# Modulation sums for two blocks over all features, in place of four blocks over half of them, and the first norm and products by pairs of blocks

## The chip, the cores and the metric

One Trainium2 chip, one of its cores. The metric is the time of one execution on the device in microseconds (us); smaller is better. Three runs of the kernel before took 2045.69, 2046.32 and 2048.83 us, median 2046.32.

## The reference, cut to what matters

A backbone of two layers over 512 latent and 256 context tokens with 1024 features each. Each layer turns a conditioning vector into six modulation vectors per stream (latent and context), and uses the first two to shift and scale the normed tokens before one wide projection:

```
mod_x = silu(c)     @ ada_w[layer] + ada_b[layer]      # ada_w: 1024 x 6144
mod_c = silu(c_ctx) @ ada_w[layer] + ada_b[layer]
sh1, sc1, g1, sh2, sc2, g2 = split(mod, 6)             # 1024 = 8 blocks of 128 features each
u = (rms_norm(x, norm1_g) * (1 + sc1) + sh1) @ w_in    # all three mixers read u
x = x + g1 * (mixers(u) @ w_out)
x = x + g2 * experts(rms_norm(x, norm2_g) * (1 + sc2) + sh2)
```

The mixers are a Fourier group, a bidirectional chunkwise mLSTM and a latent attention; the experts are a choice of 16. All is computed in 32 bits.

## The kernel before, in words

Tokens lie with features on the partitions: eight blocks of 128 features by 768 tokens, two blocks to a tile (`XB = 2`, tiles X0 to X3). The program is one long trace of instructions; a planner with a cost model of its own puts them into one queue per engine, by program order among what it takes to be ready, and each engine then works its queue in order. Transfers from memory are issued by SyncE's queue, in order too.

*The modulation.* `ada_w` is 24 MB a layer and is read in pieces of 1 MB. `ada(l, j, h)` (L462) takes one: it holds half of the input features (`h`: four blocks of 128) for four output blocks (`j`: 0 to 11, 48 output blocks in all). Sixteen products (two TensorE instructions each, so x32 in the rows) of `cs` (32 columns, two of them in use: latent and context) with 128 columns of the piece add up in one bank of the accumulation memory (`sm`, two buffers), with output block `g` on partitions 32g. For `h = 0` ScalarE copies the bank to `arow`; for `h = 1` VectorE adds the bank to `arow` (L481). At the start of the next call `ada_end` (L484) turns `arow` with one product against a selection matrix (`sel`, 8 columns), VectorE adds the bias into the tile `mod[l][j]` (L492), and for the blocks of a scale `gain` (L500) adds 1 and multiplies by the norm's weight (L505, L506).

*The start.* Layer 0 needs the first 16 output blocks at once: `j = 2, 3` are the scale, `j = 0, 1` the shift. Their eight pieces come through four buffers `raw` (pool `ada0`), behind the tokens (`X`) in SyncE's queue. `scale(i)` (L544) has VectorE multiply a pair of blocks by the row's norm `r` and the scale, giving `t1`. `norm(i)` (L550) has ScalarE add the shift and round to the high part `hH`, and VectorE form the low part `hL`, which is put in the place of the pair's X tile. `product(mt, i)` (L583) adds a pair's share to a group of output columns: 12 products (`hH` and `hL` with the weights' high part `wH`, then `hH` with the low part `wL`). Two groups run in this way, `MT_MISC` and `MT_QK`; `begin` (L578) loads their weights and has ScalarE and GpSimd split them. The order is: the scale of `j = 2` (both halves), `scale(0)`, `scale(1)`, the shift of `j = 0`, with `begin` between its halves, `norm(0)`, the sums of `j = 3`, products and sums of `j = 1` mixed in, and pairs 2 and 3 at the end (L587 to L621). What follows uses one more pool in the place of `ada0`, so its first load (`masks`, L625) and GpSimd's first clearing (`va`, L677) wait until the last `raw` has been read.

*The rest of the modulation.* The other 40 calls are fillers (L531 to L536): one is put into each group of the projection (`group`, L568) and into every third step of the attention (L1144), 24 in layer 0 (its `j` 4 to 11, and layer 1's `j` 0 to 3) and 16 in layer 1. Their pieces come through the ring `arr` by halves of 512 KB.

The experts behind each mixer stage stream their weights, three matrices of 4 MB for each of 16 experts.

## Time and profile before

| what | value |
|---|---|
| median of three runs | 2046.32 us |
| the profiled execution, its own time | 2048.57 us |
| its span (first to last instruction) | 2046.6 us |
| TensorE busy | 1876.3 us (92%) |
| VectorE, ScalarE, GpSimd busy | 860.6, 679.0, 305.3 us |
| granted TensorE clock, mean | 0.979 |
| start (tokens, first modulation, first two groups) | to 56.7 us |
| mixers of layer 0, experts of layer 0 | to about 480 us, to about 1109 us |
| mixers of layer 1, experts of layer 1 | to about 1510 us, to the end |

Times in the trace count from the span's start. A row of the timeline merges neighbours of one form: start, time to the end of the last, engine, line, operation, output and inputs, count, and in brackets how long the engine had idled before and what ended it. `big` and `sm` are banks of the accumulation memory. TensorE rows overlap by the drain of a product, so the cost of a row in a dense stream is the distance between starts. L285 and L296 are helpers (any product, any copy): go by the tiles.

### The profile page before, as it was taken

What the parts mean: (1) busy time and instruction counts of PE and PEld (TensorE: products, weight loads), DVE (VectorE), ACT (ScalarE), POOL (GpSimd) and SP (SyncE); (2) the same over time, 40 slices, a digit from 0 to 9 for tenths busy, and PEclk for the clock granted to TensorE, in tenths of its full rate; (3) what the DMA queues carried; (4) which work ended last, traced back from release to release, by engine and by line L of the source; (5) the groups of instructions that cost most, each with busy time, mean ns of one, the idle gap of its engine ahead of it and who ended that gap; (6) DMA issues with size and microseconds to landing.
All of it is one profiled execution on the core that took longest, in us unless ns stands there. A gap on an engine that the chain in (4) does not pass through costs nothing. (4 is left out here: it accounts for less than half of the span.)

```text
span 2046.6 us, 51022 instructions
## 1 busy us (share of the span) xinstructions
PE 1876.3 (92%) x22499; PEld 1285.5 (63%) x22499; DVE 860.6 (42%) x1921; ACT 679.0 (33%) x1343; POOL 305.3 (15%) x253
## 2 busy tenths in 40 slices
PE   7999999999799999999999899999968888788887
PEld 4878878887465555556554687788745444444443
DVE  4645767751323322331423756777431332212322
ACT  3534556653221121121213553556521111111113
POOL 2232232323000000000001322233320000000000
PEclk9999999999899999999999899999989999999998
DMA  8344233432899899899894334332359999999993
GB/s 313 109 131 141 84 121 127 156 127 84 320 415 362 341 390 350 334 377 366 332 342 139 121 128 149 114 117 73 125 199 405 405 404 410 417 411 405 415 423 142
DMA packets 111056, 528.13 MB, mean 258 GB/s; under 512 B 11668, under 2 KB 22676, under 8 KB 68852
## 3 DMA queue, kind: packets, MB, share of 16 engines
q1 hardware_dynamic: 107764, 514.39, 65.9%
q0 software_dynamic: 3072, 10.49, 1.8%
q8 instruction: 177, 2.90, 0.6%
q14 instruction: 43, 0.35, 0.0%
HBM read 514.29 MB, written 10.53 MB: 256 GB/s over the span
## 5 line engine op out<-in xcount | busy, mean ns | idle before, releaser
L285 PE MATMUL big<-raw,x 128*32 128x256 f32 x5440 | 315.7, 383 | 14.5 <-DMA raw<-in_eg 13.3
L285 PE MATMUL big<-raw,h 128*32 128x256 f32 (+1 forms) x4640 | 287.6, 391 | 29.3 <-DMA raw<-in_ed 27.8
L285 PEld LDWEIGHTS big<-raw,x 128*32 128x32 f32 x5440 | 169.3, 110 | 140.9 <-DMA raw<-in_eg 23.0
L285 PEld LDWEIGHTS big<-raw,h 128*32 128x32 f32 x4640 | 153.4, 110 | 154.3 <-DMA raw<-in_ed 39.1
L1405 DVE TENSOR_TENSOR yf<-big,gw 128x768 f32<-128x768 f32 (+1 forms) x30 | 24.7, 825 | 524.7 <-PE big L285 524.7
L293 POOL TENSOR_TENSOR wL<-arr,wH 128x1024 fp32r<-128x1024 f32 (+1 forms) x59 | 139.7, 2372 | 440.8 <-ACT wH L296 291.3
L1318 POOL DMA_INDIRECT xe<-hd,gx x32 | 29.4, 919 | 870.7 <-PE sm L289 817.9
L296 ACT ACTIVATE h<-sm 128x384 f32<-128x384 f32 (+1 forms) x48 | 23.5, 524 | 382.0 <-PE sm L289 382.0
L285 PE MATMUL big<-arr,x 128*32 128x256 f32 x2400 | 138.0, 380 | 12.1 <-DMA arr<-in_eu 12.1
L296 ACT ACTIVATE y<-yq 32x256 fp32r<-32x256 f32 x300 | 124.3, 414 | 4.9
L285 PEld LDWEIGHTS big<-arr,x 128*32 128x32 f32 x2400 | 76.4, 110 | 69.6 <-DMA arr<-in_eu 12.0
L285 PE MATMUL big<-hH,wH 128*128 128x512 f32 (+1 forms) x328 | 117.1, 368 | 2.1 <-ACT hH L555 2.1
L296 ACT ACTIVATE yq<-yf 128x768 fp32r<-128x768 f32 (+1 forms) x30 | 22.1, 737 | 291.3 <-DVE yf L1405 291.3
L285 PE MATMUL big<-X,wH 128*128 128x512 f32 (+1 forms) x328 | 111.0, 359 | 0.8 <-DVE X L560 0.8
L1384 DVE SCALAR_TENSOR_TENSOR X<-sm,mod,X 128x512 f32<-128x512 f32 (+1 forms) x136 | 89.4, 700 | 45.1 <-PE sm L285 44.9
L296 ACT ACTIVATE wH<-arr 128x1024 fp32r<-128x1024 f32 (+1 forms) x65 | 66.8, 1030 | 105.4 <-PE big L285 35.9
L1094 POOL TENSOR_SCALAR pr<-pr,st 128x768 f32<-128x768 f32 (+1 forms) x80 | 67.1, 842 | 164.8 <-DVE st L1093 106.5
L1414 DVE CAST y<-yq 32x256 fp32r<-32x256 f32 x300 | 87.3, 291 | 5.0
L285 PE MATMUL big<-wL,x 128*32 128x256 f32 x1200 | 82.5, 383 | 0.9 <-DMA wL<-in_eu 0.6
L285 PE MATMUL sm<-oh,y 128*128 128x512 f32 (+1 forms) x272 | 75.9, 401 | 6.7 <-ACT y L296 6.7
L285 PE MATMUL big<-hH,wL 128*128 128x512 f32 x328 | 81.6, 351 | 0.3 <-POOL wL L293 0.3
L285 PE MATMUL big<-wH,x 128*32 128x256 f32 x1200 | 76.2, 381 | 0.1
(322 smaller groups left out, 3330.1 us busy)
## 6 DMA issues: line engine op xcount, KB each, us to landing
raw<-in_eg SPq DMA_DIRECT2D x128, 1024.0 KB
raw<-in_ed SPq DMA_DIRECT2D x112, 1024.0 KB
arr<-in_eu SPq DMA_DIRECT2D x60, 1024.0 KB
arr<-in_ada SPq DMA_DIRECT2D x80, 512.0 KB
wH<-in_eu SPq DMA_DIRECT2D x60, 512.0 KB
wL<-in_eu SPq DMA_DIRECT2D x60, 512.0 KB
arr<-in_win SPq DMA_DIRECT2D x24, 512.0 KB
raw<-in_ada SPq DMA_DIRECT2D x8, 1024.0 KB
```

The costliest lines, as they stand in the source:

```text
L285: self.nc.tensor.matmul(out, a, b, start=start, stop=stop)
L293: (eng or self.nc.vector).tensor_tensor(out=out, in0=x, in1=h.bitcast(F), op=OP.subtract)
L296: self.nc.scalar.activation(out, x, AF.Copy)
L1094: nc.gpsimd.tensor_scalar(pr[:, k0:T], pr[:, k0:T], st[:, 3:4], 1.0, op0=OP.mult, op1=OP.mult)
L1318: nc.gpsimd.indirect_dma_start(out=xe[0:cap, :], out_offset=None, in_=hd[:, :], in_offset=bass.IndirectOffsetOnAxis(ap=gx[0:cap, e:e + 1], ...
L1384: nc.vector.scalar_tensor_tensor(x, ps, self.md(l, 40 + m, s), x, op0=OP.mult, op1=OP.add)
L1405: nc.vector.tensor_tensor(out=v(yf), in0=v(ps[:, 0:n]), in1=gw[:, 0:nb, e:e + 1].to_broadcast([128, nb, 256]), op=OP.mult)
L1414: nc.vector.tensor_copy(yt[s][1][d], qs[1][i].bitcast(F))
```

## The change

A piece of `ada_w` now holds all eight blocks of input features for two output blocks (24 units `u` a layer, 1 MB each as before). The four partition groups of the bank hold the two halves of the features for each of the two blocks, and the selection matrix adds the halves, so it has 4 columns in use. Every unit is copied by ScalarE, and every unit has its own turning product and bias (on half of a `mod` tile), and `gain` where it belongs to a scale. The fillers run over units 8 to 23 (and 0 to 7 of layer 1), 40 as before. At the start of layer 0, units 4 and 0 (scale and shift of the first pair) are summed first; then pair by pair: `scale`, `norm`, the scale unit of the next pair, `product` of `MT_MISC`, the shift unit of the next pair, `product` of `MT_QK`.

```diff
-    o["ada"] = g["ada_w"].reshape(L, 2, 4, 128, 12, 512).transpose(0, 4, 1, 3, 2, 5).reshape(L, 12, 2, 128, 2048)
+    o["ada"] = g["ada_w"].reshape(L, KD, 128, 24, 256).transpose(0, 3, 2, 1, 4).reshape(L, 24, 128, 2048)
...
-            sel[32 * i + j, 2 * i + j] = 1.0
+            sel[32 * i + j, 2 * (i % 2) + j] = 1.0
...
-    def ada(self, l, j, h, pool=None):
+    def ada(self, l, u, pool=None, raw=None):
...
         ps = self.small()
         for k in range(4):
             for g in range(4):
-                self.mm(ps[32 * g:32 * g + 32, 0:128], self.cs[:, 4 * h + k, :], raw[k // 2][:, k % 2 * 512 + g * 128:k % 2 * 512 + (g + 1) * 128], k == 0, k == 3)
-        if h == 0:
-            self.arow = self.sb.tile([128, 128], F, name="arow", tag="arow", bufs=2)
-            self.copy(self.arow, ps[:, 0:128])
-        else:
-            nc.vector.tensor_tensor(out=self.arow, in0=self.arow, in1=ps[:, 0:128], op=OP.add)
-            self.ended = l, j
+                h, b = g // 2, g % 2
+                self.mm(ps[32 * g:32 * g + 32, 0:128], self.cs[:, 4 * h + k, :], raw[h][:, 256 * k + 128 * b:256 * k + 128 * b + 128], k == 0, k == 3)
+        self.arow = self.sb.tile([128, 128], F, name="arow", tag="arow", bufs=2)
+        self.copy(self.arow, ps[:, 0:128])
+        self.ended = l, u
 
     def ada_end(self):
...
-        pt = self.small()[:, 0:8]
-        self.mm(pt, self.arow, self.sel[:, 0:8], True, True)
-        bias = self.vslice(l, V_ADAB + 4 * j, 4).unsqueeze(2).to_broadcast([128, 4, 2])
-        self.nc.vector.tensor_tensor(out=self.mod[l][j], in0=pt.rearrange("p (b s) -> p b s", s=2), in1=bias, op=OP.add)
-        if j % 6 // 2 == 1:
-            self.gain(l, j // 6, j % 2)
+        pt = self.small()[:, 0:4]
+        self.mm(pt, self.arow, self.sel[:, 0:4], True, True)
+        bias = self.vslice(l, V_ADAB + 2 * u, 2).unsqueeze(2).to_broadcast([128, 2, 2])
+        x = self.mod[l][u // 2][:, u % 2 * 2:u % 2 * 2 + 2, :]
+        nc.vector.tensor_tensor(out=x, in0=pt.rearrange("p (b s) -> p b s", s=2), in1=bias, op=OP.add)
+        if u % 12 // 4 == 1:
+            g = self.vslice(l, (V_N2 if u // 12 else V_N1) + u % 4 * 2, 2)
+            nc.vector.tensor_scalar(x, x, 1.0, None, op0=OP.add)
+            nc.vector.tensor_tensor(out=x, in0=x, in1=g.unsqueeze(2).to_broadcast([128, 2, 2]), op=OP.mult)
...
                 if l == 0:
-                    for h in range(2):
-                        self.ada(0, 2, h, ap)
+                    self.ada(0, 4, ap)
+                    self.ada(0, 0, ap)
                     self.ada_end()
-                    scale(0)
-                    scale(1)
-                    self.ada(0, 0, 0, ap)
                     begin()
-                    self.ada(0, 0, 1, ap)
-                    self.ada_end()
-                    norm(0)
-                    for h in range(2):
-                        self.ada(0, 3, h, ap)
-                    product(MT_MISC, 0)
-                    self.ada_end()
-                    norm(1)
-                    scale(2)
-                    scale(3)
-                    self.ada(0, 1, 0, ap)
-                    product(MT_QK, 0)
-                    product(MT_MISC, 1)
-                    self.ada(0, 1, 1, ap)
-                    product(MT_QK, 1)
-                    self.ada_end()
-                    late = (2, 3)
                 else:
                     begin()
-                    late = range(KD // XB)
-                for i in late:
-                    if l > 0:
-                        scale(i)
+                for i in range(KD // XB):
+                    scale(i)
                     norm(i)
+                    if l == 0 and i < KD // XB - 1:
+                        self.ada(0, 5 + i, ap)
                     product(MT_MISC, i)
+                    if l == 0 and i < KD // XB - 1:
+                        self.ada(0, 1 + i, ap)
+                        self.ada_end()
                     product(MT_QK, i)
```

## Rows read from the trace of the kernel before

**Rows 1.** Busy time by stretch: start:end us, length, then busy us (count) per engine.
```profile
core 0: us, PE busy (x) PEld busy (x) DVE busy (x) ACT busy (x) POOL busy (x), PEclk, DMA share, GB/s
56.00:235.00 179.00, 172.60 (x1418) 151.99 (x1417) 106.99 (x240) 82.77 (x160) 45.88 (x26) 0.98 0.36 117
235.00:430.00 195.00, 184.71 (x1507) 157.91 (x1508) 140.84 (x314) 120.42 (x253) 62.46 (x70) 0.99 0.38 129
600.00:700.00 100.00, 100.00 (x1616) 58.14 (x1608) 33.95 (x70) 20.80 (x45) 2.74 (x3) 1.00 0.99 379
1109.00:1310.00 201.00, 188.59 (x1435) 151.58 (x1435) 125.83 (x275) 94.79 (x185) 49.31 (x31) 0.96 0.37 123
1310.00:1452.00 142.00, 135.04 (x983) 114.53 (x982) 108.10 (x216) 91.81 (x173) 48.88 (x43) 1.00 0.29 92
```
**Rows 2.** The same view of the start.
```profile
25.50:29.40 3.90, 1.08 (x32) 0.84 (x32) 3.90 (x9) 2.17 (x3) 2.54 (x2) 0.98 1.00 414
29.40:36.10 6.70, 6.44 (x45) 5.02 (x45) 4.40 (x10) 4.32 (x9) 2.16 (x1) 0.50 1.01 413
36.10:46.20 10.10, 10.10 (x136) 8.30 (x136) 5.83 (x15) 0.28 (x1) 2.01 (x2) 1.00 0.33 118
36.00:38.00 2.00, 2.00 (x39) 1.59 (x39) 0.68 (x2) 0.00 (x0) 0.00 (x0) 0.97 1.00 395
38.00:40.00 2.00, 2.00 (x24) 1.63 (x26) 1.71 (x7) 0.00 (x0) 0.00 (x0) 1.00 0.21 84
```
**Rows 3.** Timeline of TensorE in the start.
```profile
24.09 0.39 PE L285 MATMUL sm<-sel,arow 128*128 128x8 f32 x2 [0.48 <-DVE arow L481]
24.41 1.08 PE L285 MATMUL sm<-raw,cs 128*32 128x128 f32 x32
26.93 1.08 PE L285 MATMUL sm<-raw,cs 128*32 128x128 f32 x32 [1.45 <-DMA raw<-in_ada]
29.66 0.59 PE L285 MATMUL sm<-sel,arow 128*128 128x8 f32 x2 [1.65 <-DVE arow L481]
...
32.05 0.80 PE L285 MATMUL big<-hH,wH 128*128 128x512 f32 x1
...
46.23 0.28 PE L285 MATMUL sm<-sel,arow 128*128 128x8 f32 x2
46.44 0.62 PE L285 MATMUL sm<-arr,cs 128*32 128x128 f32 x10
47.52 0.50 PE L285 MATMUL big<-hH,wH 128*128 128x512 f32 x1 [0.46 <-ACT hH L555]
...
52.38 0.39 PE L285 MATMUL big<-hH,wH 128*128 128x512 f32 x1
...
54.47 0.40 PE L285 MATMUL big<-hH,wH 128*128 128x512 f32 x1
...
56.66 0.64 PE L285 MATMUL sm<-arr,cs 128*32 128x128 f32 x16
```
**Rows 4.** Timeline of VectorE and ScalarE in the start.
```profile
24.92 0.17 DVE L506 TENSOR_TENSOR mod<-mod,vec 128x8 f32<-128x8 f32 x1
25.12 4.29 DVE L548 SCALAR_TENSOR_TENSOR t<-X,mod,big 128x512 f32<-128x512 f32 x8
29.33 0.28 DVE L481 TENSOR_TENSOR arow<-arow,sm 128x128 f32<-128x128 f32 x1
47.51 4.32 DVE L560 SCALAR_TENSOR_TENSOR X<-t,mod,hH 128x512 fp32r<-128x512 f32 x8 [0.79 <-ACT hH L555]
...
25.73 1.99 ACT L296 ACTIVATE wH<-arr 128x1024 fp32r<-128x1024 f32 x2
```
**Rows 5.** All instructions on the tile `arow`: durations, and waits of its users.
```profile
L285 PE MATMUL sm<-sel,arow x48: 170/256/380, 24.1 to 1450.1; 128*128 128x8 f32 x48
L296 ACT ACTIVATE arow<-sm x24: 253/277/279, 22.8 to 1373.7; 128x128 f32<-128x128 f32 x24
L481 DVE TENSOR_TENSOR arow<-arow,sm x24: 257/280/288, 23.7 to 1385.8; 128x128 f32<-128x128 f32 x24
```
**Rows 6.** What TensorE waited for from 60 to 435 us: total, times, longest.
```profile
PE sm L289 <- ACT G L803: 3.7, 1, 3.7
PE big L285 <- ACT pr L1092: 2.5, 3, 1.8
PE sm L285 <- ACT arow L296: 0.4, 1, 0.4
```

More of the change, by code (lines that the diff above doesn't have):

```diff
@@ L228, with __init__ @@
 class _Filler:
-    def __init__(self, f, layer, j, h):
-        self.f, self.layer, self.j, self.h = f, layer, j, h
+    def __init__(self, f, layer, u):
+        self.f, self.layer, self.u = f, layer, u
     def __call__(self):
-        self.f(self.layer, self.j, self.h)
+        self.f(self.layer, self.u)
 class _Kernel:
@@ L460, in conditioning @@
         nc.vector.tensor_tensor(out=cs, in0=cs, in1=c, op=OP.mult)
-    def ada(self, l, j, h, pool=None):
+    def ada(self, l, u, pool=None, raw=None):
         nc = self.nc
         self.ada_end()
-        src = self.io["ada"][l, j, h]
+        src = self.io["ada"][l, u]
         if pool:
@@ L470, in ada @@
             raw = [raw[:, 0:1024], raw[:, 1024:2048]]
-        else:
+        elif not raw:
             raw = [self.piece(src[:, i * 1024:(i + 1) * 1024]) for i in range(2)]
@@ L487, in ada_end @@
             return
-        (l, j), self.ended = self.ended, None
-        pt = self.small()[:, 0:8]
-        self.mm(pt, self.arow, self.sel[:, 0:8], True, True)
-        bias = self.vslice(l, V_ADAB + 4 * j, 4).unsqueeze(2).to_broadcast([128, 4, 2])
-        self.nc.vector.tensor_tensor(out=self.mod[l][j], in0=pt.rearrange("p (b s) -> p b s", s=2), in1=bias, op=OP.add)
-        if j % 6 // 2 == 1:
-            self.gain(l, j // 6, j % 2)
+        (l, u), self.ended = self.ended, None
+        nc = self.nc
+        pt = self.small()[:, 0:4]
[7 more added lines that the diff above has]
+            nc.vector.tensor_tensor(out=x, in0=x, in1=g.unsqueeze(2).to_broadcast([128, 2, 2]), op=OP.mult)
     def md(self, l, b, s):
         return self.mod[l][b // 4][:, b % 4, s:s + 1]
-    def gain(self, l, which, p):
-        nc = self.nc
-        x = self.mod[l][2 + 6 * which + p]
-        g = self.vslice(l, (V_N2 if which else V_N1) + 4 * p, 4)
-        nc.vector.tensor_scalar(x, x, 1.0, None, op0=OP.add)
-        nc.vector.tensor_tensor(out=x, in0=x, in1=g.unsqueeze(2).to_broadcast([128, 4, 2]), op=OP.mult)
     def attention(self, l):
@@ L531, in attention @@
             if l == 1:
-                self.fillers = [_Filler(self.ada, 1, j, h) for j in range(4, 12) for h in range(2)]
+                self.fillers = [_Filler(self.ada, 1, u) for u in range(8, 24)]
             self.s3 = P("s3")
@@ L535, in attention @@
             if l == 0:
-                self.fillers = [_Filler(self.ada, a, j, h) for a in range(L) for j in (range(4, 12) if a == 0 else range(4)) for h in range(2)]
+                self.fillers = [_Filler(self.ada, a, u) for a in range(L) for u in (range(8, 24) if a == 0 else range(8))]
             hH, hL = [], []
```

1 line of the change is left out of this document (removed).

## The prediction

> **What bounds the kernel now.** I read the busy time by stretch first [rows 1]. In the two mixer stages TensorE is busy 172.6 of 179, 184.7 of 195, 188.6 of 201 and 135.0 of 142 us: it sets the pace there, and VectorE (60 to 76%) and ScalarE (46 to 65%) follow. In the expert stages (one stretch of 100 us stands for them) the DMA share is 0.99 at 379 GB/s: transfers set the pace. The change touches no byte of those, so it can win or lose only in the mixer stages, and what it does there shifts all that follows by the same amount.
>
> Then the start, up to 56.66 us, where the first two groups end [rows 3]. Here TensorE isn't the pace everywhere. From 25.5 to 29.4 us it is busy 1.08 of 3.90 us while transfers run at 414 GB/s, and from 29.4 to 36.1 us the granted clock is 0.50, the lower of its two levels (1.2 of 2.4 GHz) [rows 2]. The reader is to see two waits in [rows 3]: 1.45 us for a piece of `ada_w` and 1.65 us for VectorE's sum into `arow`; that sum, 0.28 us long, ran only at 29.33 because eight scalings of 4.29 us stood ahead of it in VectorE's queue [rows 4]. The first product on tokens starts at 32.05. Transfers drop from 395 to 84 GB/s at 38 us: the eight pieces have landed then, and the 18 us that follow are TensorE's own work.
>
> **The start, step by step.** Take TensorE from 24.41 us, when the first scale has been turned. Its work to the end of the two groups: eight products of a pair at 54.47 - 52.38 = 2.09 us, 16.7; six sums at 1.08, 6.5; three turns at 46.44 - 46.23 = 0.21, 0.6; and half a filler (16 of 32 instructions at 1.08), 0.55 [rows 3]. That is 24.4 of the 32.25 us. Of the other 7.9, waits take 1.45 + 1.65 + 0.46 = 3.6 [rows 3], the lower clock half of 6.44 busy us, 3.2 [rows 2], and 1.1 is left for the gaps where TensorE changes between 32 and 128 columns of weights.
>
> After the change the pair's scale and shift need two pieces in place of four, and both have landed by then, since the first scale's two pieces do now. VectorE can begin the first pair after the bias of unit 0: 24.92 + 0.17 + one more 0.17, 25.3. A pair's scaling takes 4.29 / 2 = 2.15 and its low part 4.32 / 2 = 2.16 [rows 4]. The first `hH` needs one scaling and one ScalarE pass, some 1.4 us: 26.7 if the two weight splits (1.99 us [rows 4]) don't stand ahead of it on ScalarE, 28.4 if they do. So the first product starts at 26.7 to 28.4, four to five us earlier than 32.05. TensorE meanwhile has the sums of units 5 and 1, of which the later piece lands where the fourth does now, at 26.9. I put its idle time at 2.2 us: 28 - 24.4 less one sum is 2.5, less what part of the second sum fits. Behind that it is never short of work: VectorE needs 4.3 us for a pair and some 0.6 for the mods, TensorE 4.2 for the products, 2.2 for sums and 0.4 for turns.
>
> The sum at full clock: 16.7 + 6.5 + seven turns 1.5 + gaps 1.1 + idle 2.2 = 28.0, so the groups end at 52.4 in place of 56.66; the half filler (0.55) is still to do. The start gains 3.7 us. Bounds: no idle, 5.9 us; idle 3 us and the lower clock for some 10 us of work (5 us), a loss of 2. I take 3.7, since between 25.5 and 29.4 TensorE would be busy for some 2.5 us in place of 1.08, and no row of the start shows the clock falling after a stretch as busy as that.
>
> The Trainium skill ("TensorE: Matmul & The Clock Gate", "Why this matters for your kernels") says the same of direction: gaps between bursts of matmuls bring the half clock back, and keeping the engine at work avoids it. The trace agrees, with 0.50 right behind the emptiest 3.9 us [rows 2]; by the rule the 3.2 us come back, and the sum below is +0.3; were the clock to fall all the same, it would be +3.5.
>
> Covered and costed at nothing: `masks` and GpSimd's first clearing wait for the last `raw`, which now is read in pair 2 in place of pair 1, but by my sum still at some 40 to 46 us, and nothing needs them before the last pair of `MT_MISC` ends near 50. If that cover fails, up to 2 us. SyncE's queue carries the same eight pieces, the fifth to the eighth still waiting for a buffer, each freed by the first sums, so the last lands near 38 as now. The norm's broadcast `r` keeps its `big` bank for longer, until the last scaling at about 42, while the third group can't start before its weights' ring is free, at the end of `MT_MISC`.
>
> **The rest, step by step.** Before, 40 fillers have 20 turns; after, 40. The 20 added cost 0.21 us each where TensorE is dense [rows 3]: 4.2 us. The row that gives the price has 8 columns, the new turn has 4, and no row has that form. From below: nothing, where TensorE would have waited anyway; from above: 0.41, if each turn also brings a wait of 0.2 for its copy (the one such wait on record is 0.4 [rows 6]); so 0 to 8.2 for all. TensorE idles 36 of 717 us in these stretches [rows 1], so chance alone hides 5%: I take 4.0.
>
> The Trainium skill speaks against hoping for a cheaper turn: "TensorEngine Tiling (Array Packing)", "Instruction Overhead", has a matmul of one column as slow as one of 60. By it the 4 columns save nothing and the sum is the same 4.2; half the price for half the columns would make it 2.1. No run here shows it.
>
> VectorE loses 20 additions of 0.28 [rows 5] and gains 20 bias additions and 12 gain steps of 0.17 (the form of the first of [rows 4]): -5.6 + 5.4, nothing. ScalarE gains 20 copies of 0.277 [rows 5], 5.5 us over stretches where it has 327 us free [rows 1]: nothing on the path by itself. Each piece is 1 MB with the same rows, its DMAs as many. The number of changes between 32 and 128 columns stays, for a turn stands beside 128-column work.
>
> **The sum.** -3.7 + 4.0 = +0.3 us on the profiled execution: span 2046.9, its own time 2048.9 with the 2.0 us around the span. That execution lies 2.25 us above the median; put on the median the forecast is 2046.6. About 0.2% (4.1 us) is what a measurement of this kernel can tell from no change, so I forecast none.
>
> **Rivals.**
> - *Faster: the turns hide.* TensorE's queue is in order, and some of its waits in the attention are for the softmax (2.5 us in three waits on `pr` [rows 6]); work put ahead of them shortens them. With 0.5 in place of 4.0 and 4.7 in place of 3.7 at the start: 2042.1. For it: waits with ScalarE and VectorE exist in all stretches. Against: 5% of idle time is little to hide in, and the turns stand where the planner puts them.
> - *Clock: the half speed comes back at the start.* The products of the first pair trickle behind VectorE, TensorE is no busier than now until 29.4, and 3.2 of the 3.7 us are lost: 2046.3 - 0.5 + 4.0 = 2049.8. It decides if the first product starts no earlier than 28.4.
> - *Slower: the copies come late.* All 40 sums now leave through ScalarE, in place of half of them; it is 62 to 65% busy in the attention [rows 1] and works in order, the two `sm` buffers now carry 80 tiles of the fillers in place of 60, and TensorE's next user of `sm` waits. Place: 235 to 430 and 1310 to 1452 us. At 0.3 us for each of the 20 added copies the rest costs 10 in place of 4: 2052.6. Past 0.2 us a copy it decides the sign. Against: the wait on record is 0.4 us once.
> - *The gain is swallowed.* TensorE waits 3.7 us for the gate rows `G` in layer 0 [rows 6]; were that wait fixed by something other than `MT_MISC`, an earlier start would only lengthen it: 2046.3 + 4.0 = 2050.3. Against: the chain to `G` begins at the end of `MT_MISC`, which moves with the start.
>
> **How the numbers follow.** Forecast, 40%; faster, 27%; clock, 11%; late copies, 14%; swallowed, 8%. The planner sees other costs and will put instructions in another order all through the mixers, which is worth some 2 us either way in each case. The clock and swallowed cases lie at the upper edge of "no change" and give half of theirs to slower. Faster by over 0.2%: 0.27; within: 0.40 + 0.055 + 0.04 = 0.50; slower: 0.14 + 0.055 + 0.04 = 0.23. The range for 8 in 10 runs from the faster case less 2, 2040, to the slower plus a little, 2053; the likeliest case's own is 2043 to 2050.
>
> **What would show it.** In the profile after: the first `big<-hH,wH` at 26.7 to 28.4; no stretch at 0.50 between 25 and 40; the eighth pair product done near 52 to 53; 80 turn instructions behind the start, 0.2 us each in a dense stream; 48 copies to `arow` and no addition. The mark to compare is the start of the last instruction of a mixer stage less the start's gain: it should be some 2.5 us longer in layer 0 (12 turns) and 1.7 in layer 1 (8). It is wrong if the start gains under 1 or over 6 us, or if the rest costs under 1 or over 7.

## The result: slower by 0.85%

The changed kernel took 2063.65 us (median of four, 2061.70 to 2068.91), the kernel before beside it 2046.01; the ratio is 1.0085 [1.0067, 1.0103]. The forecast was 2046.6 with a range up to 2053. The profiled execution took 2063.2 us (span 2061.0, clock 0.979) against 2048.57 (2046.6, 0.979): 14.4 us more span. Both steps of the sum failed: the start lost some 6 us where 3.7 were to be gained, and the mixer stages lost 9 (7.4 in layer 0, 1.7 in layer 1) where 4.0 were priced.

Marks in the two traces, in us from the span's start:

| mark | before | after | later by |
|---|---|---|---|
| first product on tokens | 32.05 | 27.28 | -4.8 |
| ScalarE first reads the second group's bank (`cv`): end of the start | 59.6 | 65.4 | 5.8 |
| router weights of layer 0 are asked for: end of its mixers | 427.9 | 441.1 | 13.2 |
| last group of layer 1's projection is read (`cv`) | 1183.4 | 1195.6 | 12.2 |
| router weights of layer 1 are scaled (`wg`): end of its mixers | 1459.0 | 1472.9 | 13.9 |
| last block of `x` written | 1973.0 | 1988.4 | 15.4 |

The busy time by stretch after. The first two rows answer the first two of [rows 1], the others those of [rows 2]:

```profile
core 0: us, PE busy (x) PEld busy (x) DVE busy (x) ACT busy (x) POOL busy (x), PEclk, DMA share, GB/s
65.40:245.60 180.20, 171.89 (x1394) 151.14 (x1392) 104.15 (x238) 81.79 (x161) 40.80 (x25) 0.97 0.36 118
245.60:441.10 195.50, 182.38 (x1509) 157.56 (x1509) 138.45 (x318) 120.00 (x259) 61.68 (x70) 0.99 0.37 124
...
25.50:29.40 3.90, 1.38 (x3) 0.79 (x3) 3.04 (x4) 3.90 (x7) 2.75 (x2) 1.00 1.02 424
29.40:36.10 6.70, 5.01 (x20) 3.57 (x24) 3.71 (x4) 0.18 (x1) 2.37 (x1) 1.00 0.10 43
36.10:46.20 10.10, 8.63 (x123) 6.78 (x116) 5.06 (x12) 2.97 (x7) 0.00 (x0) 1.00 0.71 247
36.00:38.00 2.00, 2.00 (x34) 1.52 (x29) 0.00 (x0) 0.13 (x1) 0.00 (x0) 1.00 0.00 0
38.00:40.00 2.00, 2.00 (x17) 1.62 (x20) 0.94 (x4) 0.15 (x1) 0.00 (x0) 1.00 0.57 131
```

TensorE did 20 instructions between 29.4 and 36.1 us, where it had done 45, and the transfers, at 413 GB/s in that stretch before, fell to 43 and then to 0: the pieces of `ada_w` couldn't be fetched, because their buffers weren't read. (The clock's first record in this trace is at 37.8 us; the 1.00 ahead of it is no measurement, and the durations below tell the clock.) TensorE's timeline of the start, as in [rows 3]:

```profile
22.83 0.59 PE L285 MATMUL sm<-sel,arow 128*128 128x4 f32 x2 [0.39 <-ACT arow L296]
23.34 1.94 PE L285 MATMUL sm<-raw,cs 128*32 128x128 f32 x32
25.68 0.59 PE L285 MATMUL sm<-sel,arow 128*128 128x4 f32 x2 [0.40 <-ACT arow L296]
27.28 0.79 PE L285 MATMUL big<-hH,wH 128*128 128x512 f32 x1 [1.01 <-ACT hH L549]
29.61 0.80 PE L285 MATMUL big<-X,wH 128*128 128x512 f32 x1 [1.54 <-DVE X L554]
...
32.10 0.58 PE L285 MATMUL big<-X,wH 128*128 128x256 f32 x1 [1.48 <-DVE X L554]
...
35.81 1.94 PE L285 MATMUL sm<-raw,cs 128*32 128x128 f32 x32
...
38.63 0.28 PE L285 MATMUL sm<-sel,arow 128*128 128x4 f32 x2
...
42.82 0.50 PE L285 MATMUL big<-hH,wH 128*128 128x512 f32 x1 [1.01 <-ACT hH L549]
...
53.35 0.28 PE L285 MATMUL sm<-sel,arow 128*128 128x4 f32 x2
53.56 1.08 PE L285 MATMUL sm<-raw,cs 128*32 128x128 f32 x32
```

The first product came at 27.28, as forecast. Then TensorE waited twice for VectorE's low part (L554, writes `X`), and the next piece, unit 5, was summed only at 35.81, behind 13 of the 24 product instructions of the first pair; 1.94 us for 32 instructions in place of 1.08 is the lower clock. The other engines in the same stretch, as in [rows 4]:

```profile
22.49 18.86 SPq L469 DMA_DIRECT2D raw<-in_ada  x4
...
24.05 1.80 DVE L542 SCALAR_TENSOR_TENSOR t<-X,mod,big 128x512 f32<-128x512 f32 x3
...
26.65 5.11 POOL L293 TENSOR_TENSOR wL<-arr,wH 128x1024 fp32r<-128x1024 f32 x2 [26.23 <-ACT wH L296]
27.26 5.85 DVE L554 SCALAR_TENSOR_TENSOR X<-t,mod,hH 128x512 fp32r<-128x512 f32 x4 [0.40 <-ACT hH L549]
...
38.95 0.16 DVE L492 TENSOR_TENSOR mod<-sm,vec 128x4 f32<-128x4 f32 x1 [5.85 <-PE sm L285]
...
42.80 2.21 DVE L554 SCALAR_TENSOR_TENSOR X<-t,mod,hH 128x512 fp32r<-128x512 f32 x4 [0.79 <-ACT hH L549]
```

Four low parts took 5.85 us for the first pair and 2.21 for the second. The difference is what ran beside them: GpSimd's two weight splits, from 26.65 to 31.76. And VectorE stood idle for 5.85 us before 38.95, waiting for the turn of unit 5.

All instructions on the tile `arow` (shortest, median and longest ns, first and last start), as in [rows 5]: 48 copies and no addition, as forecast, and a turn no cheaper with four columns than with eight (256 ns; in the dense stream above, 53.35 to 53.56, 0.21 us):

```profile
L285 PE MATMUL sm<-sel,arow x96: 167/252/376, 22.8 to 1464.2; 128*128 128x4 f32 x96
L296 ACT ACTIVATE arow<-sm x48: 252/277/281, 22.5 to 1400.4; 128x128 f32<-128x128 f32 x48
```

And what TensorE waited for in layer 0's mixers (total, times, longest), as in [rows 6]. The gate rows and the copy cost what they did (3.7 and 0.4 us before); the waits for the softmax (`st`, `pr`) are longer, 6.7 us in all in place of 4.4:

```profile
PE sm L289 <- ACT G L780: 3.5, 1, 3.5
PE big L285 <- DVE st L1067: 2.4, 1, 2.4
PE big L289 <- ACT pr L1069: 2.1, 4, 0.9
...
PE big L285 <- ACT pr L1069: 1.6, 3, 0.7
...
PE sm L285 <- ACT arow L296: 0.4, 1, 0.4
```

### The profile page after: what moved, and what is told of

Read it like the earlier page. It is cut to its first block, busy times and chain, and to the rows that moved or that the text cites. A ratio compares the mean times of both kernels' runs of the same rounds, so it can differ in the third digit from the quotient of the medians.

```text
span 2061.0 us, 51154 instructions
## 1 busy us (share of the span) xinstructions
PE 1886.8 (92%) x22547; PEld 1293.3 (63%) x22547; DVE 864.6 (42%) x1937; ACT 684.2 (33%) x1367; POOL 301.5 (15%) x253
## 5 line engine op out<-in xcount | busy, mean ns | idle before, releaser
L1295 POOL DMA_INDIRECT xe<-hd,gx x32 | 29.4, 919 | 869.7 <-PE sm L289 813.4
## 6 DMA issues: line engine op xcount, KB each, us to landing
wH<-in_eu SPq DMA_DIRECT2D x60, 512.0 KB, 13.2
```

The source lines that it names most:

```text
L1295: nc.gpsimd.indirect_dma_start(out=xe[0:cap, :], out_offset=None, in_=hd[:, :], in_offset=bass.IndirectOffsetOnAxis(ap=gx[0:cap, e:e + 1], ...
```

## The experiments

All but the changed kernel were timed in five rounds, each on one chip beside the kernel before. One table for all: the ratio with its interval; the end of the start; the length of layer 0's mixers from there, with the time at the lower clock inside it, and the length less half of that time (at a granted 0.50 a sum takes 1.94 us in place of 1.08, so nearly half of such time is lost); the same for layer 1's mixers, from the last `cv` to `wg`, so corrected; and the experts of layer 1 (last `shift` to last `x`). All but the ratio come from one profiled execution.

| run | ratio | start | layer 0 | at lower clock | corrected | layer 1, corrected | experts 1 |
|---|---|---|---|---|---|---|---|
| before | 1 | 59.6 | 368.3 | 10.2 | 363.2 | 273.9 | 454.8 |
| s1 | 1.0040 [1.0024, 1.0056] | 59.0 | 373.2 | 17.1 | 364.7 | 273.4 | 460.0 |
| s2 | 1.0038 [1.0025, 1.0050] | 59.8 | 371.4 | 17.1 | 362.9 | 275.0 | 460.8 |
| n1 | 1.0021 [1.0010, 1.0031] | 58.2 | 373.5 | 20.5 | 363.3 | 274.2 | 454.0 |
| t1 | 1.0022 [1.0007, 1.0036] | 59.8 | 371.3 | 13.7 | 364.5 | 274.1 | 455.6 |
| b1 | 1.0084 [1.0069, 1.0099] | 59.1 | 375.2 | 17.1 | 366.7 | 275.9 | 461.5 |
| d1 | 1.0059 [1.0040, 1.0078] | 67.1 | 369.6 | 10.2 | 364.5 | 274.3 | 461.1 |
| a1 | 1.0011 [0.9999, 1.0022] | 58.7 | 365.2 | 6.8 | 361.8 | 273.2 | 460.9 |
| a2 | 1.0018 [1.0005, 1.0032] | 60.5 | 364.0 | 6.8 | 360.6 | 273.9 | 460.8 |
| a4 | 1.0014 [1.0003, 1.0026] | 60.9 | 367.9 | 13.7 | 361.1 | 273.6 | 460.7 |
| v1 | 0.9998 [0.9989, 1.0007] | 62.2 | 366.5 | 10.2 | 361.4 | 273.4 | 454.4 |
| after | 1.0085 [1.0067, 1.0103] | 65.4 | 375.7 | 13.7 | 368.9 | 275.6 | 454.7 |
| d2 | 1.0083 [1.0057, 1.0110] | 59.1 | 379.5 | 20.5 | 369.3 | 277.6 | 462.2 |
| f1 | 1.0081 [1.0062, 1.0100] | 58.9 | 375.6 | 17.1 | 367.1 | 278.5 | 462.1 |
| p1 | 1.0047 [1.0029, 1.0064] | 61.3 | 372.3 | 10.2 | 367.2 | 278.8 | 454.9 |
| o1 | 1.0053 [1.0033, 1.0073] | 60.9 | 375.3 | 17.1 | 366.8 | 277.7 | 454.6 |
| a3 | 1.0050 [1.0035, 1.0066] | 58.9 | 375.9 | 17.1 | 367.4 | 278.0 | 455.1 |
| h1 | 1.0019 [1.0006, 1.0031] | 60.4 | 368.7 | 6.8 | 365.3 | 275.5 | 456.6 |
| h2 | 1.0048 [1.0035, 1.0062] | 65.4 | 370.3 | 6.8 | 366.9 | 275.5 | 454.7 |
| d3 | 1.0063 [1.0049, 1.0077] | 58.6 | 372.0 | 13.7 | 365.2 | 276.6 | 460.5 |

The corrected columns are the ones to trust: four kernels with the start and fillers of before (before, s1, s2, n1) agree within 1.8 us in them, while their raw lengths of layer 0 differ by 5.2, with the time at the lower clock. Each is still one execution, so a difference of under some 2 us says little; those of n1, h1, h2 and d3 lie 3.8 to 4.6 us below the medians of their kernels.

### Which half of the change: d1, d2

d1 has the new start and the old fillers, d2 the old start and the new fillers; both layouts of `ada_w` and a selection of 4 more columns are carried for it.

```diff
+    old = g["ada_w"]...; new = g["ada_w"]...   # start of one layout, fillers of the other
-        self.sel = sb.tile([128, 664], F, name="sel")
+        self.sel = sb.tile([128, 668], F, name="sel")
```

> The changed start with the old fillers (the first eight pieces in the new layout, the other 40 as before). By the marks of the two profiles the start loses 5.7 us (third group's first product at 62.91 in place of 57.23) and the rest 8.7. If the two parts are independent: 2046 + 5.7 = 2052, ratio 1.003. Rival, that the start's delay drags the planner's order of all that follows with it: 2056 or more, and the rest longer although its fillers are those of before.

> The start of before with the new fillers (two blocks over all features, a copy and a turn for each of 40). If the fillers are what lengthens the rest: 2046 + 8.7 = 2055, ratio 1.004, with a start that ends at 57.2 as before. If only the price of 20 added turns at 0.21 counts: 2050. If the rest was lengthened by the later start alone: 2046 to 2047.

Measured: 1.0059 and 1.0083, both above what was expected. Each half loses by itself. d1's start ends at 67.1 us, 7.5 later than before, and its mixers are as before; d2's start is that of before, and its mixers are 5.8 us longer in layer 0 and 3.5 in layer 1 (corrected, against the mean of the four unchanged, 363.5 and 274.1). Each total also holds some 6 us in the experts of layer 1, which the change itself doesn't have (454.7); that is taken up last.

### The start: p1, o1, a1, a3

p1 takes GpSimd out of the way: the low parts of the first two weights' splits go to VectorE.

```diff
-            def weights(mt):
+            def weights(mt, eng=nc.gpsimd):
...
-                begun[mt] = self.big(), weights(mt)
+                begun[mt] = self.big(), weights(mt, None if l == 0 else nc.gpsimd)
```

> The changed kernel with the low parts of the first two groups' weights formed by VectorE in place of GpSimd. Theory of the lock: VectorE's first two low parts took 2.30 and 2.57 us in place of 0.75 and 0.48 because GpSimd's two splits ran beside them; without those, VectorE has two more instructions of about 1 us but the four low parts of the first pair end some 2 us earlier, and the start some 2 to 4 us: 2060 to 2062, with low parts at 0.75 and 0.48. Theory of the order: the sums of unit 5 still stand behind the first products in TensorE's queue, and the start gains under 1.5 us: 2062 to 2063.

o1 leaves the splits and puts the sums ahead of the work that waits:

```diff
-                    self.ada(0, 4, ap)
-                    self.ada(0, 0, ap)
+                    for u in (4, 0, 5, 1):
+                        self.ada(0, u, ap)
                     self.ada_end()
                     begin()
...
-                    if l == 0 and i < KD // XB - 1:
-                        self.ada(0, 5 + i, ap)
+                    if l == 0 and i < KD // XB - 2:
+                        self.ada(0, 6 + i, ap)
...
```

> The changed kernel with the sums of units 4, 0, 5 and 1 all ahead of the first products, and units 6, 2, 7, 3 one pair earlier than in the changed kernel. Theory of the order (each pair's scale and shift are summed only after the products of the pair before, so sum, copy, turn, bias, scaling and norm stand in one chain per pair): the start ends 4 to 7 us earlier, at 56 to 59, and the time is 2057 to 2060. Theory of the lock: GpSimd's splits still run beside the first low parts, so these still take over 2 us each and the gain is 2 us or less: 2061 or more.

Both held in kind. p1's start ends at 61.3, 4.1 us earlier than the changed kernel's. VectorE's timeline in p1:

```profile
26.84 1.22 DVE L293 TENSOR_TENSOR wL<-arr,wH 128x1024 fp32r<-128x1024 f32 x1
27.98 0.74 DVE L554 SCALAR_TENSOR_TENSOR X<-t,mod,hH 128x512 fp32r<-128x512 f32 x1
28.67 1.23 DVE L293 TENSOR_TENSOR wL<-arr,wH 128x1024 fp32r<-128x1024 f32 x1
29.82 1.53 DVE L554 SCALAR_TENSOR_TENSOR X<-t,mod,hH 128x256 fp32r<-128x256 f32 x3
```

The same low part takes 0.74 us, and VectorE does a split in 1.22 where GpSimd needs 5.11 for two. o1's start ends at 60.9 although its first product comes as late as 33.0: the buffers are read in time, and the transfers go on at 367 GB/s between 29.4 and 36.1 us, as the busy time by stretch of o1 has it:

```profile
core 0: us, PE busy (x) PEld busy (x) DVE busy (x) ACT busy (x) POOL busy (x), PEclk, DMA share, GB/s
...
29.40:36.10 6.70, 5.89 (x45) 4.83 (x46) 5.45 (x11) 4.28 (x7) 3.05 (x2) 1.00 0.97 367
```

GpSimd's splits are still there (33.05 to 38.21), and now the second pair's low parts run beside them and take as long as the first pair's did in the changed kernel, in VectorE's timeline of o1:

```profile
33.71 5.85 DVE L554 SCALAR_TENSOR_TENSOR X<-t,mod,hH 128x512 fp32r<-128x512 f32 x4 [0.79 <-ACT hH L549]
```

So o1 recovers its 4.5 us by the order of the sums alone, and an early first product was not the point. a3 does both, with the new fillers; a1 does both, with those of before.

> The changed kernel with both faults of its start taken out (sums ahead, splits of the first two weights on VectorE) and its own fillers. Start as in a1: the second group ends at 58.5 to 59.5. Against a1 it shows the fillers alone: if these cost what all kernels with them lost so far, corrected for the lower clock, 4.7 us in layer 0 and 3.7 in layer 1, wr stands at 428 to 434, the time at +0.2 to +0.5%. If most of that was the start's, the marks are those of before within 2 us.

> The new start with both of its faults taken out, and the fillers of before: the sums of units 4, 0, 5 and 1 stand ahead of the first weights' splits, those of 6, 2, 7 and 3 one pair earlier, and the low parts of the first two weights' splits are on VectorE in place of GpSimd. If the two causes are the whole loss of the start, the second group ends at 56 to 58 us (cv0, 59.6 before) and the time is 0.1 to 0.2% below before. If the start is bounded by the transfers of the eight pieces and TensorE's own work all the same, 60 to 61 as in each of the two alone, and the time is 0 to 0.2% above.

Their starts end at 58.9 and 58.7; a2, a4 and h1, which appear below with the same start, end theirs at 60.5, 60.9 and 60.4, with sums of 1.94 us in place of 1.08. The nine runs with the start of before end it between 58.2 and 59.8. With both causes gone most of the loss is gone, with fast sums all of it, and of the 3.7 us next to nothing is won (a1 was to reach 56 to 58). The two causes hide each other: p1 and o1 each recover 4.1 and 4.5 us, both together 4.5 to 5.0 with sums as slow as theirs and 6.5 to 6.7 with fast ones. a3 also shows that the rest is not the start's fault: it still runs at 1.0050.

### The rest: turn, bank, copy, order

t1 issues every turn twice into one bank. b1 gives a filler's second call all that a new filler has, but the copy. f1 is d2 with the copies of odd units on VectorE. n1 only reverses the order of the fillers.

```diff
         self.mm(pt, self.arow, self.sel[:, 0:8], True, True)
+        self.mm(pt, self.arow, self.sel[:, 0:8], True, True)                     # t1
...
+        if h == 1 and not pool:                                                  # b1
+            pt = self.small()[:, 0:8]
+            self.mm(pt, self.arow, self.sel[:, 0:8], True, True)
+            nc.vector.tensor_tensor(out=junk, in0=pt..., in1=bias, op=OP.add)
...
+        if u % 2:                                                                # f1
+            nc.vector.tensor_copy(out=self.arow, in_=ps[:, 0:128])
...
-        ... for j in range(4, 12) for h in range(2)]
+        ... for j in reversed(range(4, 12)) for h in range(2)]                   # n1
```

> The kernel before with every turning product of the modulation issued twice into the same bank: 24 more turns (4 in the start, 12 in the fillers of layer 0, 8 in those of layer 1), no copy, no bias and no use of a bank more. If a turn costs its place in TensorE's queue alone, 0.21 us each: the router mark of layer 0 moves by 3.4 us (to 431.3), that of layer 1 by 5.0 (to 1464), time +0.25%. If the added turns bring more than themselves (a change of tile shape, the clock), the first mark moves by 6 us or more. If the loss of the new fillers lies in what comes with the turn (copy, one more bank of sm, bias), this one stays at +3.4.

> The kernel before with everything in a filler's second call that the new one has, but the copy: a further turn at its start, with a bank of sm of its own and a bias addition that reads it (20 of each; the results go to a tile that nothing reads). If the bank and the turn behind a filler are the loss, wr of layer 0 moves by 5 us or more and the mixers of layer 1 by 3 or more (275.6 before). If the loss is in the copies or in the order of the halves, +2.5 and +1.7 at most.

> The kernel with the start of before and the new fillers, but with the copies of odd units on VectorE, so that ScalarE has the same 20 copies as before and VectorE 20 copies in place of 20 additions of the same size. If ScalarE's added copies cost the time (the rival of the late copies), the 10.7 us that the new fillers lost at the router mark of layer 0 (438.6 against 427.9) shrink to the 2.5 us of the 12 turns, 430 to 431. If the turns and the further bank of sm cost it, the mark stays at 436 to 439 and the time at +0.6 to +0.9%.

> The kernel before with the fillers of each layer in reverse order (j 11 to 4 in place of 4 to 11): the same instructions in the same number, so only which piece stands where, and so the planner's order, differs. If the planner's order and the clock's behaviour alone can cost what the new fillers cost, some mark at the end of a mixer stage moves by more than 4 us against the kernel before (router weights of layer 0 at 427.9 us, wg of layer 1 at 1459.0). If the loss comes from the turns and copies, both marks stay within 1.5 us and the time within 0.1%.

- n1 missed its bound of 1.5 us: the marks moved by 3.8 and 3.9 us, with the corrected lengths unmoved. But s1, in the order of before, has the first mark at 432.2 too: a mark of one execution holds some 4 us of clock. n1's time is 0.21% longer all the same, and where these 4 us lie its trace does not settle.
- t1: the added bare turns cost 1.0 us in layer 0 and nothing in layer 1 (corrected), less than the 2.5 and 1.7 of 0.21 each; its time, +0.22%, is what was expected of the turns, but no longer than that of n1, which adds no work.
- b1: with a bank and a reader of its own the same turn costs 3.2 and 1.8; its first mark moved by 6.4 us, past the 5 expected of the bank, layer 1 by 2.0, short of the 3. By its time b1 lost more, 0.45% beside s1 and s2, which have its longer transfers too: as much as d2. It keeps VectorE's 20 additions, which the new fillers don't have, and 3.4 us of its loss in layer 0 are lower clock (17.1 us against 10.2); what the rest is, isn't shown.
- f1: taking the added copies off ScalarE gave 2.2 us in layer 0 and nothing in layer 1 (278.5 against d2's 277.6) nor in time (1.0081 against 1.0083), so the copies are not what d2 lost; its mark of 434.5 lay between the two expectations.

A further loss showed in a wait. In layer 1's mixers TensorE waited for pieces of `ada_w` for 1.8 us before (1.6 to 2.2 in the kernels with old fillers), 3.2 in the changed kernel (the row below, from its waits) and up to 4.8 (a3):

```profile
PE sm L285 <- DMA arr<-in_ada: 3.2, 3, 1.4
```

Two neighbouring rows of TensorE's timeline show how, in the changed kernel's layer 1:

```profile
1223.57 0.41 PE L285 MATMUL sm<-arr,cs 128*32 128x128 f32 x4 [1.05 <-DMA arr<-in_ada]
1224.68 1.07 PE L285 MATMUL sm<-arr,cs 128*32 128x128 f32 x28 [0.70 <-DMA arr<-in_ada]
```

Four instructions run, then TensorE waits again for the rest of one sum. A filler's piece comes in two transfers of 512 KB. Before, the first half holds the first eight products (`raw[k // 2]`); the diff reads `raw[h]` with `h` from the inner loop, so the third product already needs the second half. h1 and h2 put the columns in the order in which the sum reads them; the instructions are the same, but the planner puts them into another order in the queues. h1 is a3 with that, h2 the changed kernel with that alone:

```diff
-    o["ada"] = ....transpose(0, 3, 2, 1, 4).reshape(L, 24, 128, 2048)
+    o["ada"] = ....transpose(0, 3, 2, 1, 4)[:, :, :, [0, 1, 4, 5, 2, 3, 6, 7]].reshape(L, 24, 128, 2048)
...
-  raw[h][:, 256 * k + 128 * b:256 * k + 128 * b + 128]
+  raw[k // 2][:, 512 * h + 256 * (k % 2) + 128 * b:512 * h + 256 * (k % 2) + 128 * b + 128]
```

> a3 with the columns of a piece laid so that the first half holds the first eight products of a sum and the second half the rest, as in the kernel before; the instructions are the same. In the changed kernel each sum reads both halves from its first four products on, so it waits for the second transfer at once. If that is a part of the loss: TensorE's waits for arr from ada_w in layer 1, 3.1 to 5.1 us in all kernels with the new fillers and 1.6 to 2.2 in those with the old, fall to about 2, and the mixers of layer 1 (cv1 to wg, 279 us) shorten by 2. If the loss lies in the turns and copies, nothing moves by more than 1 us.

> The changed kernel with one thing altered: the columns of a piece laid so that its first half holds the first eight products of a sum (as in h1). Its start stays as faulty as it was. If the order of the halves is the loss of the fillers, as a3 against h1 has it (368.7 in place of 375.9 us from the second group's end to the router weights, 275.5 in place of 279.7 in the mixers of layer 1), the time falls by 7 to 11 us against the changed kernel, to +0.3 to +0.5% above before: what is left is the start's 6 us and 1 to 3. If it isn't, +0.8% stays.

a3 to h1: 1.0050 to 1.0019; changed kernel to h2: 1.0085 to 1.0048. Both say some 7 us, 6.4 and 7.6 of 2049. The mixers of layer 0 shorten by 7.2 and 5.4 us, those of layer 1 by 4.2 and 1.8. TensorE's waits for the pieces in layer 1 fall as expected, from 4.8 to 2.2 us in h1 (the row) and from 3.2 to 1.8 in h2:

```profile
PE sm L285 <- DMA arr<-in_ada: 2.2, 3, 1.0
```

TensorE's timeline at one filler of the projection, the same in both, in a3 and then in h1:

```profile
75.49 0.41 PE L285 MATMUL sm<-arr,cs 128*32 128x128 f32 x4
77.11 1.07 PE L285 MATMUL sm<-arr,cs 128*32 128x128 f32 x28 [1.21 <-DMA arr<-in_ada]
```
```profile
77.00 1.08 PE L285 MATMUL sm<-arr,cs 128*32 128x128 f32 x32
```

Of a3's loss in layer 0 only 2.1 us is in the corrected length; the other 5.1 is the lower clock, 17.1 us of it against 6.8 (13.7 against 6.8 in the pair of h2). But 10 to 20 us of it occur in unchanged work too (before, s1, s2, n1), so that the waits brought it is not shown. The waits themselves make up 3.8 of the 11.4 us by which the mixers of both layers shorten from a3 to h1 (1.2 in layer 0), and 1.4 of 7.2 from the changed kernel to h2 (none in layer 0). That the order of the columns is worth some 7 us is shown, twice; how much of it is the second transfer, how much the clock, and how much the planner's other order stays open: n1 moved the time by 0.21% by order alone.

d3 is d2 with the halves in order (and the table 64 bytes longer in place of 16): the added turns, banks and copies by themselves.

> The start of before with the new fillers, pieces with the halves in order, and the table 64 bytes longer: the 20 added turns, banks, bias additions and copies alone. By the forecast they cost 4.0 us (2.5 in layer 0, 1.7 in layer 1), +0.2%: wr near 430.4. If with the halves in order they hide, as h1 hints (368.7 and 275.5 against 368.3 and 275.6), wr is at 427 to 429 and the time within 0.1%. If the copies or turns bring waits of their own, wr is above 433.

Corrected, 1.7 us in layer 0 and 2.5 in layer 1 against the unchanged four; with h1 against a1, a2 and a4 (4.1 and 1.9) and h2 against d1 (2.4 and 1.2) the mean is 2.7 and 1.9. The mark of 430.6 is the forecast's 430.4. The time, +0.63%, is above the 0.2% expected, but holds the longer table: beside s1 and s2 (+0.39% in the mean) it is +0.24%, 4.9 us.

### The 6 us of the wider table: a2, a4, s1, s2, v1

Every experiment with a wider table or one more tile had 460 to 462 us in the experts of layer 1. a2 (672 columns) and a4 (680) are a1 with the table padded; s1 (672) and s2 (696) are the kernel before with nothing else changed:

```diff
-        self.sel = sb.tile([128, 664], F, name="sel")
+        self.sel = sb.tile([128, 672], F, name="sel")
```

> The kernel a1_ahead_split_old with its table of constants 672 columns wide in place of 668. All four kernels that held both layouts had 668 columns (2672 bytes a partition, no multiple of 32), the others 664, and their experts of layer 1 took 461 to 462 us at 402 to 409 GB/s, in place of 455 at 408 to 415. If the four columns moved the tiles that the transfers write to a worse address, the experts of layer 1 come back to 455 us and the time falls by 6 us, to 0.1 to 0.25% below the kernel before. If mixing the layouts or chance cost it, it stays at 461 and +0.1%.

> The kernel before with its table of constants 672 columns wide in place of 664 (32 bytes a partition more, nothing reads them). Nothing is computed in another way, and every tile that is allocated behind the table lies 32 bytes further. If that is what took 6 us in the experts of layer 1 of every experiment whose tiles were moved by 16 or 32 bytes (d1, d2, f1, a1, a2, b1: 461 to 462 us in place of 455), those experts take 461 here at a lower rate of transfers in the same busy share, and the time is +0.3%. If it was the mixing of layouts, nothing moves.

> a1 with the table 680 columns wide, 64 bytes more than before. If tiles moved by a multiple of 64 bytes are as good as those of before, the experts of layer 1 are back at 455 us, and with a1's mixers (424 against 427.9 at the router weights, 1453.7 against 1459.0) the time is 0.1 to 0.3% below before. If any move costs the 6 us, it stays at +0.1%.

> The kernel before with its table 696 columns wide: 128 bytes a partition more, in place of s1's 32. If what counts is the place of the tiles by multiples of 128 bytes, the experts of layer 1 take 455 us as before and the time is that of before within 0.15%. If any longer table does it, they take 460 to 461 and the time is +0.3 to +0.4% as in s1.

The guesses on multiples of 32, 64 and 128 bytes all missed: the kernel before loses 0.40% and 0.38% by a table that is 32 or 128 bytes longer, with the same instructions in the same order in every queue. Less that, d1's start alone costs 0.20% and d2's fillers alone 0.44%. (a2 could not tell anything: in the built programs the tiles behind a table of 668 columns lie where those behind one of 672 do, so a1 and a2 are one program in all but the width of the table.) The busy time of one stretch in the experts of layer 1, columns as above, in the kernel before and then in s1, with the same share of transfers (1.02) and another rate (the last number):

```profile
1700.00:1850.00 150.00, 124.68 (x1900) 66.37 (x1904) 39.30 (x86) 25.08 (x54) 4.48 (x5) 1.00 1.02 412
```
```profile
1700.00:1850.00 150.00, 123.18 (x1904) 65.00 (x1904) 34.19 (x73) 22.86 (x50) 3.58 (x4) 1.00 1.02 407
```

The median time of a packet of 8 KB, over the some 42,030 in a trace's transfer records, is 309 ns in the ten kernels with the tiles where before has them (before, n1, t1, v1, after, p1, o1, a3, h1, h2) and 313 in the ten others, b1 among them, whose table is that of before and which moves them by one small tile. In the allocation of the built programs the four `raw` buffers that lie behind the table begin at byte 85,760, which is 335 times 256, and are 8192 bytes apart; in s1 and b1 at 85,792, in s2 at 85,888, neither a multiple of 256. The Trainium skill ("DMA: Bandwidth & Descriptors", "How a descriptor splits into AXI transactions") has a descriptor cut at multiples of 256 bytes, with one more transaction where it doesn't start on one; its account is of the bytes that are read, and the tiles that moved here are written. The packets' times agree in direction. That 256 is the step was not tried: no run moved the buffers by 256 bytes.

Only layer 1 pays. From the router weights of layer 0 to the last `cv` of layer 1, a stretch that holds the experts of layer 0, the ten kernels with the longer packets take 755.6 us in the mean and the ten others 756.0. There TensorE is busy for 100.00 of 100 us ([rows 1], 600 to 700), in layer 1's experts for 124.68 of 150: the slower transfers cost time where TensorE is not full.

v1 is the mended start with the fillers of before and no wider table; two products of four columns turn each unit of the start.

```diff
-        self.mm(pt, self.arow, self.sel[:, 664:668], True, True)
+        self.mm(pt, self.arow, self.sel[:, 0:4], True, False)
+        self.mm(pt, self.arow, self.sel[:, 4:8], False, True)
```

> The version that the runs point to: the mended start of a1 (blocks by pairs, sums ahead, the first two weights' splits on VectorE) with the fillers of before, and no wider table, since the start's units are turned by two products that add up in one bank, with the selection of before (four columns each; 8 turns more, 1.7 us). Mixers as a1, a2 and a4 (365.2, 364.0 and 367.9 us from the second group to the router weights, 368.3 before), experts of layer 1 back at 455 as in all kernels with a table of 664 columns: 2 to 5 us below before, -0.1 to -0.25%. If the start's units or the two layouts themselves cost the 6 us, the experts take 461 and the time is +0.1 to +0.2%.

The experts are back at 454.4, so mixing the layouts cost nothing; but the time is that of before, 0.9998 [0.9989, 1.0007], and not 0.1 to 0.25% below. Its start ended at 62.2, with the sums at the lower clock from 23.7 us and twice the turns, where a2 and a4, at that clock too, had 60.5 and 60.9; that took back its 2 us in layer 0. By a1, a2 and a4 (+0.11 to +0.18%) beside s1 and s2 (+0.39%) the mended start would be worth some 0.25%; why v1 shows none of it is open, and n1's order alone moved as much. No version that was run beats the kernel before.

## Why the prediction was wrong

**What bounds the kernel** stood for the mixers: TensorE sets the pace there, and what was lost there was still lost at the end. For the experts it stood in layer 1 alone; in layer 0's the row that was read for the transfers has TensorE busy for 100.00 of 100 us, and slower packets cost nothing there. The forecast does not hang on it.

**The start, -3.7 forecast, +5.8 measured.** The first product came where the forecast put it (26.7 to 28.4; 27.28). The step that failed is "behind that it is never short of work"; a term of the sum failed with it, the lower clock, put at nothing. Three things went another way:
- *GpSimd beside the low parts.* The forecast counted ScalarE's part of the weight splits and not GpSimd's, and priced a pair's low part at 2.16 us from [rows 4]. The change moves the first low parts beside GpSimd's splits; before, scalings stood there. A scaling has one operand in `big`; a low part reads both `t` and `hH` from the memory of the tiles, and the four took 5.85. p1 shows it, and o1, where the second pair's took 5.85 beside the same splits. The trace of before had the case, in other work (this form's median is 0.96 us):

```profile
66.01 2.39 POOL L293 TENSOR_TENSOR wL<-arr,wH 128x1024 fp32r<-128x1024 f32 x1 [6.10 <-PE big L285]
66.57 2.65 DVE L322 SCALAR_TENSOR_TENSOR ex<-cv,ex 128x768 f32<-128x768 f32 x1 [3.53 <-ACT ex L321]
```

  The Trainium skill states it ("SBUF — State Buffer", "SBUF: two separate sides"): VectorE with two inputs in that memory and a GpSimd operation that reads it take one port pair in turn, each for a whole instruction. The trace agrees: 5.85 in place of 2.21 us, and scalings with an operand in `big` at their usual speed beside the splits of before (4.29 us for eight, beside them and at 38.81 without).
- *The sums' place in TensorE's queue.* The forecast had TensorE fill its gaps with units 5 and 1. In the queue unit 5 stood behind products that waited, at 35.81, where o1 summed it at 26.51 and a1 at 24.43, and each pair became a chain of sum, copy, turn, bias, scaling, norm and product. With it went the cover that "the eight pieces have landed" by 38: SyncE issued the last four over 18.86 us, to 41.35, and `masks` was asked for at 54.7, where it had been 44.2. o1 shows it: there the last four were issued by 32.0.
- *The lower clock.* The sum of 28.0 has no term for the 3.2 us that the start of before lost at the lower level, so it takes them back. They stayed: the sums at 23.34 and 35.81 took 1.94 us, and the first record of the full clock is at 37.8. The mended start did not get them back either (a1 is at 0.50 from 28.1 to 34.9, a2 has its first record of the full clock at 36.8). Of the 9.5 us between forecast and measurement the first two hold 4.5 to 5.0 (65.4 less the 60.4 to 60.9 of the mended start with slow sums); these 3.2 and the 1.8 by which a1 and a2 differ are of the size of what is left.

**The clock rival** ("half speed comes back at the start") was right in the clock and wrong in its condition: the first product started before 28.4, and the clock was low all the same. It isn't the main cause of the loss against before: p1 and o1 had their sums at the lower clock too (1.94 us) and ended 4.1 and 4.5 us earlier. What it is worth shows in a1 and a2, whose starts differ in the clock alone: 58.7 and 60.5, some 1.8 of the 5.8 us. h2 does not separate it from the rest: its sums at 23.12 us ran at full speed (1.08 us for 32), but then its clock was at 0.50 from 25.4 to 35.7 and from 42.5 to 45.9, and its start ended at the same 65.4. Its busy time by stretch, columns as above (the clock is the third number from the end):

```profile
25.40:35.70 10.30, 6.46 (x33) 4.47 (x37) 6.24 (x7) 3.17 (x6) 5.12 (x2) 0.50 0.45 182
```

**The rest, +4.0 forecast, +9 measured.** The term itself was about right: 20 turns with their banks, bias additions and copies cost 4.6 us (2.7 and 1.9, corrected; the single pairs give 1.7 to 4.1 and 1.2 to 2.5), and by d3's time 4.9. Its grounds are in doubt: bare turns cost 1.0 of their 4.2 us (t1), those with a bank and a reader 5.0 (b1, corrected), which points at the bank and its reader, as far as single executions that differ by 1.8 us unchanged can tell. What failed is the list of what the change moves: "each piece is 1 MB with the same rows, its DMAs as many" is true and hides that a sum now needs its second transfer after four instructions. That step was priced at nothing, and the order of the columns cost 6.4 to 7.6 us (h1, h2), the time at the lower clock and the planner's other order included. That layer 1 lost the forecast's 1.7 us is luck: p1, o1 and a3, with the same fillers, stand 2.1 to 3.2 us higher there (corrected).

**The rivals.** *Late copies* (2052.6) had the sign and not the mechanism: the wait for a copy stayed at 0.4 us, and f1, without the added copies on ScalarE, gave 2.2 us in layer 0, none in layer 1 and none in time. *Faster* had the turns hide: bare ones did for the most part (t1), those with a bank did not. *Swallowed* had `G` fixed; it moved with the start, and the wait for it was 3.5 us (3.7 before).

**The sum by runs.** The changed kernel is at +0.85%. Mending the start alone gives +0.50 (a3), the halves alone +0.48 (h2), both +0.19 (h1): 3.9 us, where the forecast had 4.0 for the rest, with nothing won at the start. Some 0.35 and 0.37% for the two and 0.19 left add up to 0.91, within the intervals. The 0.19 can't be put to the turns by its size alone, since the same fillers in reverse order (n1) are at +0.21; that is why the corrected lengths are used above.

## What to carry to other kernels

When an operation moves, look at what runs beside its new place on the engine that shares its port, and search the trace for the longest duration of that form, not the median. When a layout changes, walk through the first few reads of the loop and ask which transfer each one needs; and write out where in its queue each filler will stand, since work that has landed does not fill a gap that lies ahead of it in the queue. A control that only moves tiles belongs beside any experiment that adds one: here it was worth 0.4%, half of what was to be explained. So does one that only reorders: it was worth 0.2% here, as much as the term under test.

## What the runs showed of the hardware

Unexpected: where the expert weights land decides 1.3% of the transfer rate (309 or 313 ns for a packet of 8 KB, 412 or 407 GB/s), so four more columns in a table ahead of them cost 6 us in layer 1's experts, and nothing in layer 0's, where TensorE was full. And the same program reaches its start at either clock: a1 and a2, whose starts are the same instructions, had sums of 1.08 and 1.94 us at 23 us, and ended their starts at 58.7 and 60.5.
